# Turning v and the normed scan output on VectorE, in 32x32 blocks that their DRAM stores put in place

## The chip, the cores and the metric

The kernel runs on one core of one Trainium2 chip. The time is device microseconds of one execution of the whole program. Before the change three runs took 1355.96 to 1357.52 us, with a median of 1356.4.

## What is computed

A trunk of two layers runs over 640 tokens, 128 of a prompt and 512 of a latent grid, each 1024 wide. Layer A is a chunked gMLP, layer B a gated DeltaNet in both directions with eight heads, keys and queries of 128 and values of 256. The change lies in layer B. Cut to that, the reference is:

```python
def delta_mixer(h, s0_f, s0_b, w_in, conv_w, A_log, dt_bias, norm_g, w_out):
    proj = h @ w_in
    qkv, z, ab = jnp.split(proj, [2 * KW + VW, 2 * KW + 2 * VW], axis=-1)
    qkv = jax.nn.silu(short_conv(qkv, conv_w))
    q, k, v = jnp.split(qkv, [KW, 2 * KW], axis=-1)
    ...
    o_f, s_f = gated_delta_chunked(q, k, v, g[:, :, 0], beta[:, :, 0], s0_f)
    o_b, s_b = gated_delta_chunked(flip(q), flip(k), flip(v), flip(g[:, :, 1]), flip(beta[:, :, 1]), s0_b)
    o = o_f + flip(o_b)
    o = o * lax.rsqrt(jnp.mean(jnp.square(o), axis=-1, keepdims=True) + LN_EPS) * norm_g
    y = o.reshape(B, N, VW) * jax.nn.silu(z)
    return y @ w_out, s_f, s_b
```

The recurrence wants v with tokens on the partitions; the convolution before it, and the product with z and the output projection behind it, want channels on the partitions. So v and the result o are each turned once on the way.

## The kernel before the change

Layer A takes up to about 500 us of the span, layer B's heads from about 545 to 1245, and layer B's output projection (`out_b`) the rest to 1354, with its first part among the last heads. Products of the two projections are exact to nearly f32: each is three matmuls of split operands, written by `mm3` (L235 high by high, L236 and L237 with the low parts).

Layer B is a set of Python generators, one for each step of a head: `project_head` (one of four 128-channel parts q: 0 is k, 1 is q, 2 and 3 are the halves of v; output in `xp`), `conv` (five taps along the tokens, L845 and L848, then SiLU, L851 and L853; output `cacc`, channels on the partitions), `post_k`, `post_q` and `post_v` (into the layouts that follow), `chunk` (the triangular systems of a 128-token chunk, by products in bank `pt`), `scan` (the recurrence, five steps with a forward and a backward unit each, banks `ps`), `norm_o` (the norm of o), `project_z` and `gate_z` (the gate, and the product with it), `residual`, and the gates.

`stages()` gives every generator a stretch of time, in windows: in window w (-2 to 8) stand the scan of head w, the chunks of head w+1, the projections of head w+2, and the norm and gate of head w-1, each with its begin and end in sixths of a window. `turns()` sorts the pieces by these times, and that is the order in which the code is issued. TensorE and SP (the queue that issues nearly all DMAs) keep this written order; that of VectorE, ScalarE and GpSimd is set by a scheduler. A window is about 80 us long in the profile: the k store of a head (L907) is issued at 804.62, 884.03, 963.48, 1043.96 and 1125.20.

The two steps that the change touches:

- `post_v` (L931): TensorE turns `cacc` into bank `px`, four 128x128 transposes for the latent tokens and one for the prompt (`flip`, L878, which calls `transpose`, L239). ScalarE copies them to `nat` times 0.5 (L938; SiLU was computed without its factor of one half). One store puts `nat` into the DRAM tensor `kvd` (L941), which holds k and v of a head with tokens as rows.
- `norm_o` (L1166) takes the squares of o on ScalarE, and scales o by its norm on GpSimd for heads 0 to 6 (L1182); o has tokens on the partitions. `gate_z` (L1204) then turns each half of o on TensorE, again 4 and 1, and VectorE multiplies `px` by the gate and the norm's weight into `z` (L1213). A store puts the product into `yd` (L1215), from where `out_b` loads it as `cacc` (L1247).

`scan` loads v from `kvd` (L1097, 128 KB each, four buffers), a pair ahead of each step: L1112 is the product of the state S with k and q, L1115 takes it from v, which gives r, L1125 and L1126 are the products with r, L1134 and L1140 the new state and the output. `chunk` loads k as `kn` (L961). Every DMA of SP takes one of eight semaphores in turn, and waits for the DMA that had it before, so at most eight are on their way.

Of the kernel before, what the change touches and what calls it, by code (L numbers as in the profile page):

```python
# [6 lines left out]
F32 = mybir.dt.float32  # L7
# [3 lines left out]
ALU = mybir.AluOpType  # L11
PSUM = bass.MemoryType.PSUM

P = 128
# [33 lines left out]
NORM_LEN = 1.0  # L48
CONV_AT, CONV_LEN, POST_AT, POST_LEN, NORM_AT, GATE_AT, GATE_STEP = 1.0, 1.0, 2.0, 1.0, 0.4, 1.5, 0.6
CAT, CLEN = 0.0, 0.9  # L50
CSTEP = CLEN / 40 * 4
# [22 lines left out]
def tok(c):  # L74
# [7 lines left out]
PIECES = {"scan": 24, "chunk": 40, "norm_o": 4, "gate_z": 4, "conv": 8, "post_k": 13,  # L82
          "post_q": 7, "post_v": 5, "gates": 7, "gates_e": 26, "residual": 17}


def stages():
# [5 lines left out]
    for w in range(-2, H + 1):  # L92
# [11 lines left out]
        for i, (kind, h, q) in enumerate(slots):  # L104
            i = start + i * wide
            add("project_" + kind, (h, q), i / n, (i + wide) / n, 17)
            if kind == "head":
                i += wide - 1
                add("conv", (h, q), (i + CONV_AT) / n, (i + CONV_AT + CONV_LEN) / n)
                add(("post_k", "post_q", "post_v", "post_v")[q], (h, q), (i + POST_AT) / n,  # L110
                    (i + POST_AT + (KLEN if q == 0 else POST_LEN)) / n)
        if w == -2:
# [12 lines left out]
        if at(-1):  # L125
            add("norm_o", (w - 1,), NORM_AT / n, (NORM_AT + NORM_LEN) / n)
            for j in range(2):
                add("gate_z", (w - 1, 4 + j), (GATE_AT + GATE_STEP * j) / n, (GATE_AT + 0.5 + GATE_STEP * j) / n)
    return parts
# [78 lines left out]
class Trunk:  # L208
# [421 lines left out]
    def layer_b(self):  # L630
# [4 lines left out]
        self.e_d = self.dram([P, TT, H, P], "ed")  # L635
        self.kv_d = [self.dram([P, TT, P + DV], "kvd") for _ in range(H)]
        with contextlib.ExitStack() as banks, pool("b_c") as bc:
# [11 lines left out]
            self.convw = t(bc, [P, H, 4, CONV], F32, "convw")  # L649
            nc.sync.dma_start(self.convw, a["convw"])  # L650
            self.ngT = t(bc, [P, 2], F32, "ngT")
            nc.sync.dma_start(self.ngT, a["ngT"])
# [185 lines left out]
    def conv(self, h, q):  # L838

        nc, t = self.nc, self.t  # L840
        xp = self.acc[h, q]
        acc = t(self.b2, [P, PADN], F32, "cacc")
        self.acc[h, q] = acc, xp
        w = self.convw[:, h, q]
        nc.scalar.activation(acc, xp[:, 0:PADN], AF.Copy, scale=w[:, 0:1])  # L845
        yield
        for i in range(1, CONV):
            nc.vector.scalar_tensor_tensor(acc, xp[:, i : i + PADN], w[:, i : i + 1], acc, op0=ALU.mult, op1=ALU.add)  # L848
            yield
        th = xp[:, 2 : 2 + PADN]  # L850
        nc.scalar.activation(th, acc, AF.Tanh, scale=0.5)  # L851
        yield
        nc.vector.scalar_tensor_tensor(acc, th, 1.0, acc, op0=ALU.add, op1=ALU.mult)  # L853
        if q != 1:
            self.gap(xp)
        yield
# [29 lines left out]
    def post_k(self, h, q):  # L886
# [7 lines left out]
        for c0 in (1, 0):  # L894
# [11 lines left out]
            yield  # L906
        nc.sync.dma_start(self.kv_d[h][:, :, 0:P], kn)  # L907
        for c0 in (1, 0):
# [22 lines left out]
    def post_v(self, h, q):  # L931
        nc, t = self.nc, self.t
        s, _ = self.acc[h, q]
        v = t(self.b1, [P, TT, P], F32, "nat")
        for c0 in (1, 0):
            p = self.flip(lambda c: s[:, tok(c)], c0)
            yield
            nc.scalar.mul(v[:, c0 : c0 + p.shape[1], :], p, 0.5)  # L938
            if c0:
                yield  # L940
        nc.sync.dma_start(self.kv_d[h][:, :, P * (q - 1) : P * q], v)  # L941
        yield

    def chunk(self, h, cs):
# [15 lines left out]
        kn = t(b1, [P, nt, P], F32, f"kn{nt}")  # L960
        nc.sync.dma_start(kn, self.kv_d[h][:, those, 0:P])  # L961
        pg = bank()
# [116 lines left out]
    def scan(self, h):  # L1079
# [15 lines left out]
        def load(c):  # L1095
            v = t(b1, [P, DV], F32, "v", bufs=KVB)
            nc.sync.dma_start(v, self.kv_d[h][:, c, P : P + DV])  # L1097
            return v
# [65 lines left out]
    def norm_o(self, h):  # L1164
# [14 lines left out]
        for c in range(TT):  # L1179

            if h < H - 1:
                nc.gpsimd.tensor_scalar(o[c], o[c], f[:, c : c + 1], 0.0, op0=ALU.mult, op1=ALU.add)  # L1182
            elif c % 2:
                nc.vector.tensor_scalar(o[c], o[c], f[:, c : c + 1], None, op0=ALU.mult)
            else:
                nc.scalar.activation(o[c], o[c], AF.Copy, scale=f[:, c : c + 1])
        yield

    def project_z(self, h, q):
# [14 lines left out]
    def gate_z(self, h, q):  # L1204

        nc, t = self.nc, self.t
        z2, o = self.zz[h, q], self.oo[h]
        j = q - 4
        for c0 in (1, 0):
            p = self.flip(lambda c: o[c][:, j * P : (j + 1) * P], c0)  # L1210
            yield
            sl = slice(c0 * P, (c0 + p.shape[1]) * P)
            nc.vector.scalar_tensor_tensor(z2[:, sl], p.rearrange("p c n -> p (c n)"), self.ngT[:, j : j + 1],  # L1213
                                           z2[:, sl], op0=ALU.mult, op1=ALU.mult)
        nc.sync.dma_start(self.y_d[2 * h + j], z2)  # L1215
        yield
# [204 lines left out]
```

## Time and profile before

| what | value |
|---|---|
| runs before, median (lowest to highest) | 1356.4 us (1355.96 to 1357.52) |
| the profiled execution, its own time | 1356.03 us |
| its span | 1354.2 us |
| mean granted TensorE clock | 0.99 |
| transfers: v loads (128 KB) | 72 |
| transfers: stores into `kvd` (320 KB) | 24, of which 16 are v |
| matmul instructions | 8773 |

The time is the span and 1.8 us around it. Rows of the profile have the form "line, engine, operation, output and inputs by the program's names, shapes, count", then the busy time and the mean duration. L240 is the helper that every transpose on TensorE goes through, so these are told apart by what they read: `cacc`, `o` or `nat`. A wait in brackets is the idle time of an engine just ahead of an instruction, and what ended it. In the list of groups, "x128 | 137.7, 1076" reads 128 instructions, 137.7 us of busy time, 1076 ns each.

### The profile page before, as it was taken

How to read it: one execution, taken by the hardware profiler on the slowest of the kernel's cores; microseconds unless marked ns; L12 is line 12 of the kernel's file. 1: busy time of each engine (PE TensorE's matmuls, PEld its weight loads, DVE VectorE, ACT ScalarE, POOL GpSimd, SP SyncE). 2: the span in 40 equal slices, each digit the busy share in tenths (PEclk: the TensorE clock that was granted, in tenths of full speed). 3: DMA queues.
4: the chain of work that ended last, by engine and by line, in shares of the span. 5: the costliest groups of instructions: out<-in, count | busy, mean ns of one | idle time of the engine just before them, and what ended most of it. 6: DMA issues, size and time to landing. Idle time of an engine off the chain costs nothing. (4 is left out here: it accounts for less than half of the span.)

```text
span 1354.2 us, 22812 instructions
## 1 busy us (share of the span) xinstructions
PE 1282.5 (95%) x8773; PEld 1137.3 (84%) x8773; DVE 875.7 (65%) x1655; ACT 578.7 (43%) x1352; POOL 502.0 (37%) x503
## 2 busy tenths in 40 slices
PE   7999999999999999888999999999999999999996
PEld 4688999999997887778888898999899898887785
DVE  4654744444447566798677778686787868656357
ACT  2333522222224334665545354564545546443320
POOL 0221422222223434354343536355464646520024
PEclk9999999999999999998999999999999999999999
DMA  8512233333336324142122422234233242445732
GB/s 337 168 63 93 94 125 125 125 125 125 125 125 218 118 76 145 56 140 86 50 77 73 136 78 65 100 89 153 79 125 108 85 139 88 133 141 174 261 117 78
DMA packets 90254, 163.17 MB, mean 120 GB/s; under 512 B 9089, under 2 KB 55457, under 8 KB 90017
## 3 DMA queue, kind: packets, MB, share of 16 engines
q1 hardware_dynamic: 88704, 156.99, 35.3%
q10 hardware_dynamic: 1440, 4.72, 1.0%
q8 instruction: 69, 1.13, 0.3%
q14 instruction: 41, 0.33, 0.1%
HBM read 135.97 MB, written 25.71 MB: 119 GB/s over the span
## 5 line engine op out<-in xcount | busy, mean ns | idle before, releaser
L231 POOL TENSOR_TENSOR wlo<-wraw,whi 128x256 fp32r<-128x256 f32 (+1 forms) x188 | 194.4, 1054 | 261.6 <-ACT whi L230 261.6
L235 PE MATMUL pp<-hThi,whi 128*128 128x320 f32 (+1 forms) x784 | 280.1, 357 | 0.2 <-ACT hThi L230 0.2
L237 PE MATMUL pp<-hTlo,whi 128*128 128x320 f32 (+1 forms) x784 | 244.7, 312 | 0.4 <-POOL hTlo L231 0.4
L236 PE MATMUL pp<-hThi,wlo 128*128 128x320 f32 (+1 forms) x784 | 244.1, 311 | 0.0
L230 ACT CAST whi<-wraw 128x256 fp32r<-128x256 f32 (+1 forms) x262 | 143.5, 593 | 84.6 <-PE pacc L236 57.6
L235 PE MATMUL pacc<-hThi,whi 128*128 128x320 f32 x512 | 159.6, 312 | 0.0
L237 PE MATMUL pacc<-hTlo,whi 128*128 128x320 f32 x512 | 158.3, 309 | 0.0
L236 PE MATMUL pacc<-hThi,wlo 128*128 128x320 f32 x512 | 158.2, 309 | 0.0
L848 DVE SCALAR_TENSOR_TENSOR cacc<-xp,convw,cacc 128x642 f32<-128x642 f32 x128 | 137.7, 1076 | 25.0 <-ACT cacc L845 23.6
L235 PEld LDWEIGHTS pp<-hThi,whi 128*128 128x128 f32 (+1 forms) x784 | 148.8, 190 | 3.9 <-ACT hThi L230 0.3
L236 PEld LDWEIGHTS pp<-hThi,wlo 128*128 128x128 f32 (+1 forms) x784 | 148.6, 190 | 4.0
L237 PEld LDWEIGHTS pp<-hTlo,whi 128*128 128x128 f32 (+1 forms) x784 | 147.7, 188 | 1.8 <-POOL hTlo L231 0.7
L231 DVE TENSOR_TENSOR wlo<-wraw,whi 128x1024 fp32r<-128x1024 f32 (+1 forms) x74 | 87.7, 1196 | 60.0 <-ACT whi L230 59.5
L248 POOL TENSOR_TENSOR rs<-ve,mhalf 128x1 f32<-128x1 f32 (+2 forms) x39 | 40.1, 1028 | 170.1 <-DVE ve L246 166.7
L235 PEld LDWEIGHTS pacc<-hThi,whi 128*128 128x128 f32 x512 | 96.1, 188 | 3.1 <-issue 2.2
L236 PEld LDWEIGHTS pacc<-hThi,wlo 128*128 128x128 f32 x512 | 96.1, 188 | 0.0
L237 PEld LDWEIGHTS pacc<-hTlo,whi 128*128 128x128 f32 x512 | 96.1, 188 | 0.0
L256 POOL TENSOR_SCALAR gsq<-gsq 128x320 f32<-128x320 f32 (+1 forms) x52 | 27.7, 532 | 138.4 <-ACT gsq L255 137.4
L257 DVE TENSOR_TENSOR gsq<-pacc,gsq 128x320 f32<-128x320 f32 (+1 forms) x52 | 29.1, 565 | 73.9 <-POOL gsq L256 73.8
L255 ACT ACTIVATE gsq<-pacc 128x320 f32<-128x320 f32 (+1 forms) x52 | 25.7, 498 | 106.2 <-PE pacc L237 102.3
L235 PE MATMUL pacc<-whi,hThi 128*128 128x512 f32 x160 | 63.1, 406 | 7.6 <-ACT whi L230 4.4
L1032 ACT CAST TU<-pt 128x512 f16<-128x512 f32 (+1 forms) x120 | 57.2, 525 | 26.4 <-PE pt L1029 25.5
(333 smaller groups left out, 2974.9 us busy)
## 6 DMA issues: line engine op xcount, KB each, us to landing
wraw<-in_w_b SPq DMA_DIRECT2D x48, 512.0 KB
wraw<-in_w_ada SPq DMA_DIRECT2D x37, 512.0 KB
wraw<-in_w_uz SPq DMA_DIRECT2D x32, 512.0 KB
v<-kvd SPq DMA_DIRECT2D x72, 128.0 KB
wraw<-in_a_wo SPq DMA_DIRECT2D x16, 512.0 KB
wraw<-in_b_wo SPq DMA_DIRECT2D x16, 512.0 KB
kvd<-nat SPq DMA_DIRECT2D x24, 320.0 KB
cacc<-yd SPq DMA_DIRECT2D x24, 320.0 KB
```

The costliest lines, as they stand in the source:

```text
L230: self.nc.scalar.copy(hi, src)
L231: (e_lo or self.nc.vector).tensor_tensor(lo, src, f32(hi), op=ALU.subtract)
L235: mm(out, l_hi, r_hi, start=start, stop=False)
L236: mm(out, l_lo, r_hi, start=False, stop=False)
L237: mm(out, l_hi, r_lo, start=False, stop=stop)
L248: nc.gpsimd.tensor_tensor(r, ve, self.mhalf[:, 0:n], op=ALU.pow)
L255: nc.scalar.activation(sq, u, AF.Square)
L256: nc.gpsimd.tensor_scalar(sq, sq, GB, 1.0, op0=ALU.mult, op1=ALU.add)
L257: nc.vector.tensor_tensor(sq, u, sq, op=ALU.mult)
L848: nc.vector.scalar_tensor_tensor(acc, xp[:, i : i + PADN], w[:, i : i + 1], acc, op0=ALU.mult, op1=ALU.add)
L1032: nc.scalar.copy(part, p.rearrange("p s k t (j b) -> p s (k t j) b", b=b))
```

## The change

v is turned by VectorE. Its instruction turns each 32x32 block in place in the grid of blocks, so a block's inside is right and its place is not; the store to DRAM puts the blocks in their places, 32 partitions by 20 blocks by 32 numbers, four stores for each half of v. The half that ScalarE applied is moved into the convolution's weights (one GpSimd operation at the start), and the scale of the tanh is doubled for it. `kvd` is laid out with a token's k and v in one row. The stores stand five pieces behind the transposes, and `post_v` is stretched from 1.0 to 1.4 sixths of a window.

For heads 0 to 6 the norm of o scales on ScalarE instead of GpSimd. A new step `turn_o` turns each o (128x256) with one VectorE instruction, and three pieces later writes it to a new DRAM tensor `od` with four stores (32 partitions by 8 by 32). A new step `load_o` reads it back as `oT`, channels on the partitions, in two loads of 320 KB. `gate_z` is moved from 1.5 to 4.7 sixths of the window, is one VectorE operation of 640 columns out of SBUF, and stores `yd` three pieces later. Head 7 keeps the transposes on TensorE.

```diff
+TURN_AT, TURN_LEN, LOAD_AT, TURNED_AT, VLEN = 1.6, 1.6, 3.7, 4.7, 1.4
...
+            at_gate = GATE_AT
+            if w < H:
+                add("turn_o", (w - 1,), TURN_AT / n, (TURN_AT + TURN_LEN) / n)
+                add("load_o", (w - 1,), LOAD_AT / n, (LOAD_AT + 0.4) / n)
+                at_gate = TURNED_AT
...
-        nc.scalar.activation(th, acc, AF.Tanh, scale=0.5)
+        nc.scalar.activation(th, acc, AF.Tanh, scale=0.5 if q < 2 else 1.0)
...
     def post_v(self, h, q):
...
-        v = t(self.b1, [P, TT, P], F32, "nat")
-        for c0 in (1, 0):
-            p = self.flip(lambda c: s[:, tok(c)], c0)
-            yield
-            nc.scalar.mul(v[:, c0 : c0 + p.shape[1], :], p, 0.5)
-            if c0:
-                yield
-        nc.sync.dma_start(self.kv_d[h][:, :, P * (q - 1) : P * q], v)
+        v = t(self.b1, [P, NT], F32, "nat")
+        nc.vector.transpose(v[:, P:NT], s[:, tok(1).start : tok(4).stop])
+        yield
+        nc.vector.transpose(v[:, 0:P], s[:, tok(0)])
+        for _ in range(5):
+            yield
+        rows = self.kv_d[h].rearrange("(a i) n -> i a n", i=32)
+        for b in range(4):
+            at = P * (q - 1) + 32 * b
+            nc.sync.dma_start(rows[:, :, at : at + 32],
+                              v[32 * b : 32 * b + 32].rearrange("p (a n) -> p a n", n=32))
...
-            if h < H - 1:
-                nc.gpsimd.tensor_scalar(o[c], o[c], f[:, c : c + 1], 0.0, op0=ALU.mult, op1=ALU.add)
-            elif c % 2:
+            if h == H - 1 and c % 2:
...
+    def turn_o(self, h):
...
+        for c in range(TT + 3):
+            if c < TT:
+                x = self.t(self.b0, [P, DV], F32, "ot", bufs=4)
+                nc.vector.transpose(x, o[c])
+                wait.append(x)
+            if c >= 3:
+                cols = self.o_d[h].rearrange("(b j) n -> j b n", j=32)
+                for a in range(4):
+                    at = (c - 3) * P + 32 * a
+                    nc.sync.dma_start(cols[:, :, at : at + 32],
+                                      wait[c - 3][32 * a : 32 * a + 32].rearrange("p (b n) -> p b n", n=32))
+            yield
+
+    def load_o(self, h):
+        self.turned = []
+        for j in range(2):
+            x = self.t(self.b0, [P, NT], F32, "oT", bufs=2)
+            self.nc.sync.dma_start(x, self.o_d[h][j * P : (j + 1) * P, :])
+            self.turned.append(x)
+            yield
...
     def gate_z(self, h, q):
...
+        if h < H - 1:
+            nc.vector.scalar_tensor_tensor(z2, self.turned[j], self.ngT[:, j : j + 1], z2, op0=ALU.mult, op1=ALU.mult)
-        for c0 in (1, 0):
+        for c0 in (1, 0) if h == H - 1 else ():
...
+        if h < H - 1:
+            yield
+            yield
+            yield
         nc.sync.dma_start(self.y_d[2 * h + j], z2)
```

What the change does to the order of SP, in a steady window (head 4's scan loads `kvd_4838`, while head 5's v is written to `kvd_4839`; `wraw` is a weight, `rn` and `x` belong to the residual). Before:

```order
L1097 DMA v_10920<-kvd_4838 128x256
L1097 DMA v_10922<-kvd_4838 128x256
L961 DMA kn_2046_10938<-kvd_4839 128x2x128
L701 DMA x_80_498<-rn_10805 128x256
L696 DMA rn_11020<-n_76_494 128x256
L941 DMA kvd_4839<-nat_10914 640x1x128
L1215 DMA yd_4823<-z_1739_9573 128x640
L166 DMA wraw_11095<-in_w_b 128x1024
L701 DMA x_81_499<-rn_11020 128x256
L1097 DMA v_11155<-kvd_4838 128x256
L1097 DMA v_11157<-kvd_4838 128x256
```

The same place of SP in the changed kernel, from the first of these v pairs to the second:

```order
L1110 DMA v_10930<-kvd_4838 128x256
L1110 DMA v_10932<-kvd_4838 128x256
L974 DMA kn_2039_10948<-kvd_4839 128x2x128
L710 DMA x_80_498<-rn_10821 128x256
L953 DMA kvd_4839<-nat_10743 32x20x32 x4
L705 DMA rn_11027<-n_76_494 128x256
L172 DMA wraw_11099<-in_w_b 128x1024
L710 DMA x_81_499<-rn_11027 128x256
L1214 DMA od_4845<-ot_11049 32x8x32 x4
L953 DMA kvd_4839<-nat_10928 32x20x32 x4
L1110 DMA v_11163<-kvd_4838 128x256
L1110 DMA v_11165<-kvd_4838 128x256
```

Between the pairs stand twelve small stores, where one of `kvd` and one of `yd` stood; the first store of v has moved here from ahead of the first pair, and the `yd` store has gone to the end of the window.

In window 7 (the scan of the last head, loads from `kvd_4841`) TensorE's order holds matmuls of the output projection between those of the scan; `pp` and `pt` with `kq`, `G` and `whi` or `wlo` are the projection, `ps` the scan. Before, around its fourth step:

```order
L236 MATMUL pt_14139<-whi_13814,G_2782_14170 128x512
L1125 MATMUL ps_14040<-r_14034,G_2687_13898 128x256
L1126 MATMUL ps_14040<-r_14034,G_2687_13898 128x256
L1125 MATMUL ps_14043<-r_14037,G_2687_13898 128x256
L1126 MATMUL ps_14043<-r_14037,G_2687_13898 128x256
L237 MATMUL pt_14139<-wlo_13815,kq_14148 128x512
L1112 MATMUL ps_14056<-S_14046,kq_12584 128x256 x2
L1112 MATMUL ps_14059<-S_14049,kq_12584 128x256 x2
L235 MATMUL pt_14140<-whi_13814,kq_14148 128x512
```

The changed kernel's TensorE at the same step, its first rows:

```order
L1138 MATMUL ps_14077<-r_14059,G_2680_13950 128x256
L1139 MATMUL ps_14077<-r_14059,G_2680_13950 128x256
L241 MATMUL pp_14208<-whi_13865,kq_14218 128x512
L1125 MATMUL ps_14090<-S_14080,kq_12622 128x256 x2
L1125 MATMUL ps_14093<-S_14083,kq_12622 128x256 x2
L242 MATMUL pp_14208<-whi_13865,G_2778_14240 128x512
L243 MATMUL pp_14208<-wlo_13866,kq_14218 128x512
L241 MATMUL pt_14209<-whi_13865,kq_14218 128x512
L242 MATMUL pt_14209<-whi_13865,G_2778_14240 128x512
L243 MATMUL pt_14209<-wlo_13866,kq_14218 128x512
```

The products with S are here followed by 26 matmuls of the projection, of which five are shown, before the products with r of the same step; before the change two or three stood there. On SP, 16 stores of `od` stand between the v pair of this step and that of the step ahead.

More of the change, by code (lines that the diff above doesn't have):

```diff
@@ L82 @@
 PIECES = {"scan": 24, "chunk": 40, "norm_o": 4, "gate_z": 4, "conv": 8, "post_k": 13,
-          "post_q": 7, "post_v": 5, "gates": 7, "gates_e": 26, "residual": 17}
+          "post_q": 7, "post_v": 7, "turn_o": 8, "load_o": 2, "gates": 7, "gates_e": 26, "residual": 17}
 def stages():
@@ L110, in stages @@
                 add(("post_k", "post_q", "post_v", "post_v")[q], (h, q), (i + POST_AT) / n,
-                    (i + POST_AT + (KLEN if q == 0 else POST_LEN)) / n)
+                    (i + POST_AT + (KLEN, POST_LEN, VLEN, VLEN)[q]) / n)
         if w == -2:
@@ L126, in stages @@
             add("norm_o", (w - 1,), NORM_AT / n, (NORM_AT + NORM_LEN) / n)
+            at_gate = GATE_AT
[3 more added lines that the diff above has]
+                at_gate = TURNED_AT
             for j in range(2):
-                add("gate_z", (w - 1, 4 + j), (GATE_AT + GATE_STEP * j) / n, (GATE_AT + 0.5 + GATE_STEP * j) / n)
+                add("gate_z", (w - 1, 4 + j), (at_gate + GATE_STEP * j) / n, (at_gate + 0.5 + GATE_STEP * j) / n)
     return parts
@@ L635, in layer_b @@
         self.e_d = self.dram([P, TT, H, P], "ed")
-        self.kv_d = [self.dram([P, TT, P + DV], "kvd") for _ in range(H)]
+        self.kv_d = [self.dram([NT, P + DV], "kvd") for _ in range(H)]
+        self.o_d = [self.dram([DV, NT], "od") for _ in range(H - 1)]
         with contextlib.ExitStack() as banks, pool("b_c") as bc:
@@ L650, in layer_b @@
             nc.sync.dma_start(self.convw, a["convw"])
+            nc.gpsimd.tensor_scalar(self.convw[:, :, 2:4], self.convw[:, :, 2:4], 0.5, 0.0, op0=ALU.mult, op1=ALU.add)
             self.ngT = t(bc, [P, 2], F32, "ngT")
@@ L906, in post_k @@
             yield
-        nc.sync.dma_start(self.kv_d[h][:, :, 0:P], kn)
+        nc.sync.dma_start(self.kv_d[h].rearrange("(c p) n -> p c n", p=P)[:, :, 0:P], kn)
         for c0 in (1, 0):
@@ L960, in chunk @@
         kn = t(b1, [P, nt, P], F32, f"kn{nt}")
-        nc.sync.dma_start(kn, self.kv_d[h][:, those, 0:P])
+        nc.sync.dma_start(kn, self.kv_d[h].rearrange("(c p) n -> p c n", p=P)[:, those, 0:P])
         pg = bank()
@@ L1096, in load @@
             v = t(b1, [P, DV], F32, "v", bufs=KVB)
-            nc.sync.dma_start(v, self.kv_d[h][:, c, P : P + DV])
+            nc.sync.dma_start(v, self.kv_d[h][c * P : (c + 1) * P, P : P + DV])
             return v
@@ L1187, in norm_o @@
         yield
+    def turn_o(self, h):
+        nc = self.nc
+        o = self.oo[h]
+        wait = []
+        for c in range(TT + 3):
[17 more added lines that the diff above has]
+            yield
     def project_z(self, h, q):
```

## The prediction

> **What bounds the kernel now.** I read the page first: its head and the busy shares say how much of the span TensorE, VectorE and the others work.
>
> ```profile
> span 1354.2 us, 22812 instructions
> PE 1282.5 (95%) x8773; PEld 1137.3 (84%) x8773; DVE 875.7 (65%) x1655; ACT 578.7 (43%) x1352; POOL 502.0 (37%) x503
> ```
>
> TensorE is busy for 95% of the span, so time is lost or won by what it is given to do. Those shares are a mean over different stages, so I next asked for busy times by stretch, cut at the length of one window of layer B (one head's scan, with the chunks of the next head and the projections of the one after).
>
> ```profile
> core 0: us, PE busy (x) PEld busy (x) DVE busy (x) ACT busy (x) POOL busy (x), PEclk, DMA share, GB/s
> 800.00:880.00 80.00, 78.04 (x623) 72.50 (x622) 60.46 (x129) 41.45 (x119) 36.08 (x42) 1.00 0.28 91
> 960.00:1041.00 81.00, 77.62 (x618) 72.27 (x619) 60.81 (x128) 41.72 (x120) 45.61 (x52) 1.00 0.34 109
> sum 610.00, PE 583.27 PEld 535.12 DVE 447.24 ACT 308.49 POOL 282.99; mean PE 72.91 PEld 66.89 DVE 55.91 ACT 38.56 POOL 35.37
> ```
>
> In a window TensorE idles 2 to 3.4 us of 80. VectorE has 60.8 us of 81 (75%), ScalarE half, the transfers a third. A matmul taken away here is time taken away, as long as nothing else starts to be waited for. Third, the list of what TensorE waits for, over the whole span (total us, times, longest):
>
> ```profile
> PE px L240 <- DVE cacc L853: 8.0, 4, 4.4
> PE pt L1047 <- ACT U L1038: 4.6, 6, 1.6
> PE ps L1112 <- DVE o L1140: 3.9, 5, 1.2
> PE pt L1029 <- DVE Y L1022: 3.2, 5, 0.6
> PE px L240 <- DVE z L1213: 0.7, 2, 0.5
> ```
>
> The largest wait in it stands before transposes that the change removes: TensorE waits for the convolution's output `cacc` so as to turn it. The rest are short, and all in the scan and the chunks.
>
> **TensorE's part.** The order shows 150 transposes fewer on TensorE: 80 of `cacc` for v (8 heads, two halves, 4 and 1) and 70 of `o` (heads 0 to 6, two halves, 4 and 1). The rows of the bank `px` that they fill, minimum, median and maximum in ns:
>
> ```profile
> L240 PE MATMUL px<-ident,cacc x120: 270/272/474, 575.3 to 1160.4; 128*128 128x128 f32 x120
> L240 PE MATMUL px<-ident,o x80: 270/272/331, 763.1 to 1245.1; 128*128 128x128 f32 x80
> L938 ACT ACTIVATE nat<-px x32: 257/438/602, 598.6 to 1160.9; 128x512 f32<-128x512 f32 x16, 128x128 f32<-128x128 f32 x16
> ```
>
> The 272 ns are from start to end of one; TensorE overlaps them, so the price is the distance between starts. TensorE's timeline around one group of four and one single transpose:
>
> ```profile
> 1009.26 0.31 PE L236 MATMUL pp<-hThi,wlo 128*128 128x320 f32 x1
> 1009.41 0.31 PE L237 MATMUL pp<-hTlo,whi 128*128 128x320 f32 x1
> 1009.55 0.60 PE L240 MATMUL px<-ident,o 128*128 128x128 f32 x4
> 1009.91 0.39 PE L235 MATMUL pp<-hThi,whi 128*128 128x320 f32 x1
> 1010.14 0.30 PE L236 MATMUL pp<-hThi,wlo 128*128 128x320 f32 x1
> ...
> 1011.12 0.31 PE L237 MATMUL pp<-hTlo,whi 128*128 128x320 f32 x1
> 1011.27 0.27 PE L240 MATMUL px<-ident,o 128*128 128x128 f32 x1
> 1011.30 0.39 PE L235 MATMUL pp<-hThi,whi 128*128 128x320 f32 x1
> 1011.53 0.31 PE L236 MATMUL pp<-hThi,wlo 128*128 128x320 f32 x1
> ```
>
> An undisturbed step from one start to the next is 0.15 us (1009.26 to 1009.41). From the L237 ahead of the four to the L236 behind them there are two such steps and the four transposes: 1010.14 - 1009.41 = 0.73, less 0.29 for the two steps. Around the single one it is 1011.53 - 1011.12 = 0.41, less 0.29. Four cost 0.44, one 0.12, a group of five 0.55. Thirty groups (16 of v, 14 of o) make 16.5 us, all of it on the engine that sets the pace. The Trainium skill ("VectorE: DVE Perf Modes", The three transpose paths) gives 390 ns for a 128x128 bf16 transpose on TensorE. By that figure 150 of them would be an estimated 58 us; the rows here, at 0.11 us each between its neighbours, decide.
>
> The waits for `cacc` and for z, 8.0 and 0.7 us, stand before transposes of these two kinds, and nearly all of it goes from TensorE with them. But what follows then comes earlier, and waits for the same `cacc` chain through the v store, or for ScalarE and VectorE in chunk and scan. I take half: 4 us. The ends are 0 and 8.7.
>
> **VectorE's part.** No row of before shows its 32x32 transpose; the nearest are its operations of the same widths:
>
> ```profile
> L853 DVE SCALAR_TENSOR_TENSOR cacc<-xp,cacc 128x642 f32<-128x642 f32 x32 | 27.8, 868 | 7.4 <-ACT xp L851 7.4
> L1140 DVE TENSOR_TENSOR o<-o,ps 128x256 f32<-128x256 f32 x72 | 29.9, 416 | 6.0 <-PE ps L1126 4.3 <-ACT r L1131 1.3
> L1213 DVE SCALAR_TENSOR_TENSOR z<-px,ngT,z 128x512 f32<-128x512 f32 x14 | 10.5, 750 | 7.3 <-PE px L240 7.1
> L1213 DVE SCALAR_TENSOR_TENSOR z<-px,ngT,z 128x128 f32<-128x128 f32 x13 | 4.5, 344 | 0.5 <-PE px L240 0.5
> L1118 ACT ACTIVATE o<-ps,scal 128x256 f32<-128x256 f32 x32 | 14.6, 474 | 49.3 <-DVE r L1115 49.3
> L1182 POOL TENSOR_SCALAR o<-o,rs 128x256 f32<-128x256 f32 x35 | 19.0, 559 | 0.7
> ```
>
> Per window: two times 0.75 + 0.34 for v, five times 0.42 for o, and the product with z in one operation of 640 (0.87 at most, as L853) for 0.75 + 0.34, twice: 2.2 + 2.1 - 0.4 = 3.9 us more, 60.8 to 64.7 of 79. ScalarE gains five of 0.47 for the norm and loses the two L938 pairs (a median of 0.44 each, 1.8 in all): half a microsecond more of 41.7. GpSimd loses five of 0.56. VectorE's 3.9 us in eight windows are 31 us; of a VectorE delay TensorE sees only what falls ahead of an operation it waits for. The ends are 0 and 31; its rows of waits for VectorE that stay (3.9 and 3.2) are about 1% of 610, but the delays come in the same stretches, so I take a tenth: 3 us.
>
> **SP's part.** SP issues the transfers in a written order. Per v half, four stores of 32 partitions by 20 by 32 (128-byte pieces) take the place of one; per head 20 stores of `od` and two loads come new. SP's timeline with VectorE's use of what is loaded, and from the chain of waits the time of one store and one v load:
>
> ```profile
> 1002.29 0.53 SPq L941 DMA_DIRECT2D kvd<-nat  x1
> 1004.94 0.33 SPq L1215 DMA_DIRECT2D yd<-z  x1
> 1006.90 0.96 SPq L1097 DMA_DIRECT2D v<-kvd  x2
> ```
>
> ```profile
> 1012.89 0.48 DVE L1115 SCALAR_TENSOR_TENSOR r<-ps,neg,v 128x256 f32<-128x256 f32 x1 [0.82 <-PE ps L1112]
> ```
>
> ```profile
> 1043.96 3.94 DMA kvd<-nat
> ...
> 1213.43 3.60 DMA v<-kvd
> ```
>
> A v pair issued at 1006.90 is used at 1012.89, 6.0 us later, and 3.6 are its landing: 2.4 us to spare. In the new order four `od` and four `kvd` stores stand ahead of that pair, where one store of `kvd` and one of `yd` stood: by the rows 8 x 0.53 = 4.2 us of issue for 0.9. Between the first two rows SP had nothing to issue for 2.1 us, so issue alone sets the pair back by 4.2 - 0.9 - 2.1 = 1.2, within the 2.4. Over a window 28 more transfers (6 for v, 20 stores and 2 loads of `od`) take 9 to 15 us of SP's 80. What is queued behind a store that waits for VectorE are v pairs and weights, and the weights are asked for well ahead. I take 0 for the steady windows; the other end is the last of the rivals.
>
> **The end of the scan.** In window 7 no more heads follow, and 16 of the `od` stores of head 6 stand in one row between two v pairs of the last scan:
>
> ```profile
> 1218.70 0.93 SPq L1097 DMA_DIRECT2D v<-kvd  x2
> 1223.32 2.05 SPq L1097 DMA_DIRECT2D v<-kvd  x4
> ```
>
> ```profile
> 1254.46 0.24 PE pt L237
> ...
> 1261.12 8.00 DMA cacc<-yd
> ```
>
> Before, four v loads went out together at 1223.32. Now two of them stand behind 16 stores: 5.3 us at 0.33, 8.5 at 0.53. The written order on TensorE puts 26 matmuls of the output projection there (`pp` and `pt` with L235 to L237), 0.24 each, so 6.2 us. What is left, and the reload of `o` before head 6's product, costs between 0 and 8 us; I take 3, because the next load for the output projection stands behind the same 16 stores.
>
> **The sum.** The profiled execution took 1356.03 us, 1.8 beyond its span; the median of the runs is 1356.4. 1356.0 - 16.5 - 4 + 3 + 3 = 1341.5, and 0.4 for the median: 1342. A measurement of this kernel can tell 0.2%, 2.7 us, from no change: faster is below 1353.7, slower above 1359.1.
>
> **The rivals.**
>
> *Better.* All 8.7 us of the waits go, VectorE and the end cost nothing: 1356.4 - 16.5 - 8.7 = 1331. For it: the steady windows show no wait at all before these transposes, so little has to be paid back there. Against: 97% busy leaves short chains of VectorE and ScalarE just hidden. Chance 0.10; with parts of it, 1331 to 1336.
>
> *VectorE becomes what TensorE waits for.* If the transpose costs three times the rows above, a window's v and o transposes take 13 us in place of 4.3, and VectorE is at 73 of 79. It has 20 us free in a window, so it alone sets the pace only from about five times. At three times, a sixth of the extra 8.6 us on the path in each of eight windows gives back 11: 1353, 1346 to 1360. Against: it reads and writes as many elements as its neighbours. Chance 0.10. The page named above gives 311 ns for 128x128 bf16 on VectorE, for blocks of 32x32; that is an estimated 1.24 us for 512 wide, 1.7 times the row taken here, and by it the sum would be near 1344. No run yet shows it.
>
> *The end gives it back.* Scan 7 and the reload of head 6's `o` each go through 16 stores at 0.53; if the output projection runs dry behind them, 8 + 4 us instead of 3: 1351. For it: the last row above, where the end already waits 8 us for a load of that projection. Chance 0.10.
>
> *Slower: the small stores hold SP.* No store of 128-byte pieces stands in the trace beside these; the page only counts small packets:
>
> ```profile
> DMA packets 90254, 163.17 MB, mean 120 GB/s; under 512 B 9089, under 2 KB 55457, under 8 KB 90017
> ```
>
> The change adds 64 x 640 and 140 x 256 pieces of 128 bytes, 76,800, for 10,240 of 512 bytes. Each transfer waits for the one eight before it, so at most eight are on their way. So a v pair goes out at the earliest one landing after the first of the eight stores ahead of it; with a landing of L us instead of the 4.2 that their issue takes, it is set back by 1.2 + (L - 4.2). The point from which that decides, with 2.4 to spare, is L = 5.4, where the row above has 3.9 for a store. Two v pairs of a window have such a block ahead, in seven windows: at 6.5 they lose 14 x 1.1 = 15 us against the gain of 14.5, and 1357 comes out; at 7.1, 24 us and 1366; at 8, 36 us and 1378. Against it: the DMA share of the windows is 0.28 to 0.34, so there is room for as many packets again. Chance 0.18, 1355 to 1380, with its middle at 1366. The Trainium skill ("DMA: Bandwidth & Descriptors", Specifications) asks for at least 512 B a transfer and says that below this a read-modify-write takes place. That speaks for this rival; no run yet shows a time for it.
>
> **How the numbers follow.** The forecast's own case, 1337 to 1346, has 0.52. Better 0.10, VectorE 0.10, the end 0.10, SP 0.18. The likeliest gives 1342. The range 1333 to 1358 leaves out half of the better case and three quarters of SP's: 0.05 + 0.13 = 0.18. Faster by over 0.2%: 0.52 + 0.10, of the end 0.08, of VectorE 0.06, and 0.01 of SP, 0.77. Within 0.2%: 0.02 + 0.03 + 0.03 = 0.08. Slower: 0.14 of SP and 0.01 of VectorE, 0.15.
>
> **What would show it.** Right: windows of about 78 us instead of 80 with TensorE's busy time down by 2, no px wait for `cacc` L853 but the k ones, VectorE near 65 us a window, its 512-wide transpose near 0.7 us, and SP's v pairs still issued 5 us ahead of use. Wrong: transposes on VectorE over 1.5 us for 512 columns; waits of VectorE for v (L1110) in each window; windows of 80 us with TensorE at 75; or a span from the last scan's start to the end that is more than 5 us longer. If the stores land in 2 to 4 us, the slower rival falls.

## The result, and the profile after

The changed kernel takes 1403.5 us (1403.13 to 1404.52), the kernel before 1356.2 in the same runs: a ratio of 1.0345, interval 1.0329 to 1.0362. It is 47 us slower, where 1342 was forecast. First the page's head, as before the change:

```profile
span 1401.3 us, 22752 instructions
PE 1290.9 (92%) x8623; PEld 1138.2 (81%) x8623; DVE 889.2 (63%) x1708; ACT 579.7 (41%) x1355; POOL 490.7 (35%) x469
```

TensorE has its 150 instructions fewer and is busy for 8 us longer. The list of its waits says where it stands idle, and the next rows what the new VectorE operations cost (count, busy time, mean ns):

```profile
PE ps L1138 <- ACT o L1131: 19.9, 7, 4.0
PE pt L1030 <- DVE TU L1017: 18.2, 9, 5.6
PE pt L1060 <- DVE U L1054: 9.9, 6, 2.1
```

```profile
L1208 DVE STREAM_TRANSPOSE ot<-o 128x256 f32<-128x256 f32 x35 | 14.9, 432 | 4.1 <-ACT o L1197 4.1
L1247 DVE SCALAR_TENSOR_TENSOR z<-oT,ngT,z 128x640 f32<-128x640 f32 x12 | 12.8, 1067 | 0.0
L945 DVE STREAM_TRANSPOSE nat<-cacc 128x512 f32<-128x512 f32 x16 | 11.3, 704 | 0.0
L947 DVE STREAM_TRANSPOSE nat<-cacc 128x128 f32<-128x128 f32 x16 | 4.6, 285 | 0.0
```

The wait for `cacc` ahead of the transposes is gone, and three others took its place: before the scan's products with r, and in the chunk before the product with TU and before that with U (two steps of the triangular systems). Each transpose costs about what the operations of the same width cost before (432 ns for 416, 704 for 750, 285 for 344). To see where the time went, I cut the span at the k stores of heads 3 and 7 (`nat` to `kvd`, 804.62 and 1125.20 before):

```profile
810.02 0.37 SPq L916 DMA_DIRECT2D kvd<-nat  x1
...
1156.74 0.37 SPq L916 DMA_DIRECT2D kvd<-nat  x1
```

Up to the first, the change has lost 5.4 us; over the four steady windows between them 26.1 (346.7 for 320.6); behind the second 15.6 (244.6 for 229.0). A steady window is followed on three engines. SP first, from a store of the residual to the second v pair of head 4's scan:

```profile
1021.07 0.32 SPq L710 DMA_DIRECT2D x<-rn  x1
1021.44 1.93 SPq L1214 DMA_DIRECT2D od<-ot  x4
1023.47 2.08 SPq L953 DMA_DIRECT2D kvd<-nat  x4
1025.60 1.01 SPq L1110 DMA_DIRECT2D v<-kvd  x2
```

Before the change the pair went out 0.4 us behind `x<-rn`, now 4.5 us behind it. By the trace's DMA events it landed at 1028.0 and 1028.4. The stores were not held by the limit of eight transfers: the DMA that had the first v load's semaphore before it had landed at 1023.1, 2.5 us before that load was issued. They follow `x<-rn`, for which SP had stood idle since 1013.2, because it waits for GpSimd's `rn`. SP's waits for it over the whole span (total us, times, longest), before and after:

```profile
SPq L701 <- POOL rn L700: 35.5, 9, 4.8
SPq L710 <- POOL rn L709: 81.4, 12, 11.1
```

By itself this wait need not cost anything: in the run below that loads v ahead of the stores (e_ahead) it is 107.6 us, and the windows are 20 us shorter. What is new is that eight stores stand between it and the pair. VectorE then:

```profile
1025.45 0.43 DVE L1208 STREAM_TRANSPOSE ot<-o 128x256 f32<-128x256 f32 x1
1031.31 0.95 DVE L1035 TENSOR_TENSOR Y<-pt,wm 128x128 f16<-128x128 f32 x3 [5.42 <-PE pt L1030]
1034.44 3.08 DVE L857 SCALAR_TENSOR_TENSOR cacc<-xp,convw,cacc 128x642 f32<-128x642 f32 x3 [2.18 <-ACT cacc L854]
1037.44 0.86 DVE L1128 SCALAR_TENSOR_TENSOR r<-ps,neg,v 128x256 f32<-128x256 f32 x2
```

VectorE idles for 7.6 us (5.42 and 2.18), about 5 of them with v there, and takes r 9 us after v landed, behind three Y and three convolution taps. The products with S, which r needs too, were done by 1027.5. So it is the order of VectorE's queue and not the data. Before the change the two r of this step (the first at 1012.89, shown in the prediction) ran ahead of those Y and taps:

```profile
1013.75 0.48 DVE L1115 SCALAR_TENSOR_TENSOR r<-ps,neg,v 128x256 f32<-128x256 f32 x1 [0.38 <-PE ps L1112]
1017.55 0.95 DVE L1022 TENSOR_TENSOR Y<-pt,wm 128x128 f16<-128x128 f32 x3 [3.31 <-PE pt L1017]
```

The scheduler has put them ahead of r. I take it that it reckons v late behind the small stores; what it reckons is not shown, but r stands in its old place in the runs that load v earlier (e_ahead) or have large stores (e_big).

TensorE, whose order is written by hand, stands before the product with r for the last 4.0 us of that time, and pays twice. Its row of the timeline, then the windows table, which has the granted clock in the column behind POOL; the first stretch lies ahead of the same wait one window earlier, the second behind it, the third begins within the wait of this row and ends 4.7 us behind it:

```profile
1038.47 1.22 PE L1138 MATMUL ps<-r,G 128*128 128x256 f32 x2 [4.04 <-ACT o L1131]
```

```profile
940.00:946.70 6.70, 6.70 (x75) 6.16 (x73) 0.95 (x3) 3.20 (x9) 0.65 (x1) 1.00 0.55 115
951.20:954.40 3.20, 3.20 (x10) 2.54 (x9) 2.33 (x4) 0.74 (x1) 1.88 (x2) 0.50 0.11 36
...
1036.60:1043.20 6.60, 4.73 (x13) 4.01 (x14) 5.62 (x10) 1.60 (x3) 4.18 (x5) 0.50 0.45 127
```

At these waits of 4 us the clock is 0.50 for some 3.4 and 6.8 us, and so busy time grows where work has shrunk. A shorter wait can do it too, as an earlier window of the kernel before shows: the row of the wait, then a stretch ahead of it and one behind it.

```profile
715.33 0.22 PE L1028 MATMUL pt<-Y,TU 128*128 128x64 f16 x2 [1.76 <-DVE Y L1022]
```

```profile
709.00:713.00 4.00, 4.00 (x34) 3.72 (x34) 3.50 (x6) 2.95 (x10) 2.97 (x4) 1.00 0.00 0
716.30:719.70 3.40, 3.40 (x15) 3.36 (x15) 1.68 (x6) 2.07 (x5) 0.54 (x1) 0.50 0.27 73
```

But not every such wait is followed by it: behind one of 2.21 us that ended at 925.08 in the changed kernel (before the product with TU), the clock stays at 1.00 from 925.1 to 929.0. Over the span the withheld clock is 0.025 x 1401 = 35 us against 0.01 x 1354 = 14. The Trainium skill ("TensorE: Matmul & The Clock Gate", What's actually happening) has the clock halved after an idle window of some 3.4 us; the length agrees with the stretches here, but a wait of 1.76 us was followed by it and one of 2.21 us was not.

### The profile page after: what moved, and what is told of

It reads as the page before. It is cut to its first block, busy times and chain, and to the rows that moved or that the text cites. A ratio compares the mean times of both kernels' runs of the same rounds, so it can differ in the third digit from the quotient of the medians.

```text
span 1401.3 us, 22752 instructions
## 1 busy us (share of the span) xinstructions
PE 1290.9 (92%) x8623; PEld 1138.2 (81%) x8623; DVE 889.2 (63%) x1708; ACT 579.7 (41%) x1355; POOL 490.7 (35%) x469
## 4 chain that ended last, share of the span: by engine, by line
PE 25%; DVE 15%; issue 7%; ACT 6%; POOL 3%; DMA 2%; SPq 1%; ACTq 0%; POOLq 0%; DVEq 0%
DVE cacc L857 5%; PE pp L241 5%; PE pp L242 4%; PE pp L243 4%; PE ps L1125 2%; POOL rs L254 2%; PE ps L1139 2%; DVE M L995 2%; PE ps L1138 1%; POOL wlo L237 1%; ACT junk L885 1%; ACT cacc L854 1%; PE pt L1030 1%; DVE grhs L805 1%; DMA v<-kvd 1%
## 5 line engine op out<-in xcount | busy, mean ns | idle before, releaser
L237 POOL TENSOR_TENSOR wlo<-wraw,whi 128x256 fp32r<-128x256 f32 (+1 forms) x188 | 199.3, 1081 | 322.7 <-ACT whi L236 308.9
L1035 DVE TENSOR_TENSOR Y<-pt,wm 128x128 f16<-128x128 f32 (+1 forms) x144 | 47.9, 373 | 60.6 <-PE pt L1030 60.3
L1125 PE MATMUL ps<-S,kq 128*128 128x256 f32 x256 | 67.2, 404 | 7.4 <-issue 3.5
```

Of the source, the lines that this page charges most:

```text
L237: (e_lo or self.nc.vector).tensor_tensor(lo, src, f32(hi), op=ALU.subtract)
L1035: nc.vector.tensor_tensor(yc, pair(p), pair(self.wm[:, l - 1, :, 0:nt]), op=ALU.mult)
L1125: nc.tensor.matmul(p[:, q], kq[:, c, q, :], S, start=True, stop=True)
```

## The experiments

Times are medians beside the kernel before on the same chip, with the ratio's interval. The parts of the span are those above: to head 3's k store, the four windows, and the rest; they are of the one profiled execution, which can lie 4 us from the median. Seven runs leave out part of the work or put blocks in wrong places, as their texts say (e_big, e_none, e_stores, e_tiny, e_vbig, e_obig, e_none_mp), and serve for their times alone. The code cuts are shortened.

| run | us | ratio | to head 3 | four windows | rest |
|---|---|---|---|---|---|
| before | 1356.2 | 1 | 804.6 | 320.6 | 229.0 |
| changed | 1403.5 | 1.0329 to 1.0362 | 810.0 | 346.7 | 244.6 |
| e_pin | 1388.5 | 1.0221 to 1.0267 | 805.7 | 337.3 | 245.4 |
| e_big | 1369.7 | 1.0078 to 1.0121 | 807.7 | 319.7 | 236.7 |
| e_v | 1368.9 | 1.0062 to 1.0112 | 808.5 | 322.0 | 237.6 |
| e_o | 1364.7 | 1.0039 to 1.0080 | 806.8 | 319.8 | 236.4 |
| e_none | 1351.4 | 0.9948 to 0.9991 | 803.1 | 315.0 | 231.5 |
| e_dve | 1362.4 | 1.0035 to 1.0079 | 808.3 | 322.5 | 232.3 |
| e_stores | 1419.1 | 1.0445 to 1.0485 | 812.4 | 358.4 | 247.4 |
| e_ahead | 1378.9 | 1.0143 to 1.0221 | 806.5 | 327.0 | 242.8 |
| e_tiny | 1409.3 | 1.0378 to 1.0412 | 817.7 | 350.6 | 241.6 |
| e_vbig | 1373.1 | 1.0096 to 1.0157 | 804.3 | 326.6 | 240.5 |
| e_obig | 1378.7 | 1.0144 to 1.0180 | 811.7 | 329.5 | 238.2 |
| e_actq | 1395.9 | 1.0277 to 1.0313 | 813.0 | 337.9 | 243.8 |
| e_none_mp | 1332.3 | 0.9824 to 0.9858 | 795.6 | 309.0 | 226.0 |
| e_mp | 1369.3 | 1.0086 to 1.0118 | 800.7 | 327.7 | 235.6 |
| e_ahead_mp | 1352.2 | 0.9969 to 0.9997 | 797.8 | 311.3 | 240.5 |
| e_fix2 | 1346.4 | 0.9906 to 0.9945 | 798.9 | 312.1 | 235.5 |
| e_fix3 | 1345.9 | 0.9915 to 0.9954 | 798.4 | 312.4 | 233.0 |
| e_bahead | 1353.1 | 0.9969 to 0.9998 | 803.9 | 318.9 | 228.0 |

**Order alone, large stores, and each half.** My theory was the order on VectorE (A); its rivals transport (B) and VectorE's load (C). The first run pins the order, the second takes the small stores away, the others make one half of the change.

```diff
+    # e_pin: for each VectorE instruction traced after an r
+    add_manual_dep(ins, last_r.name, NoSync)
-    # e_big: the four stores of a group, for v and for o alike
+    nc.sync.dma_start(kv_d[h].rearrange("(c p) n -> p c n", p=P)[...], v.rearrange("p (c n) -> p c n", n=P))
```

Expected of e_pin:

> The changed kernel with one constraint on VectorE's order: nothing that is written behind an r of the scan (the subtraction from v) may be queued ahead of it. Every instruction and every transfer stays. Theory A (order): the scheduler reckons the small stores slow, expects v late, and queues six Y operations and three convolution taps ahead of r in the second scan step; v had in fact landed 8 to 9.5 us before r ran. Then this kernel gets back most of the 47 us: under 1365, and TensorE's waits of 4 us before the products with r (L1138) go. Theory B (transport): the small stores hold SP and the v pairs go out late; then r waits for v in the same place, and the time stays over 1390. Theory C (VectorE's load): the transposes themselves are in the way; over 1390 as well, without waits for v.

Expected of e_big:

> The changed kernel with each group of four stores of 128-byte pieces replaced by one store of 512-byte pieces of the same bytes (the blocks' placing is left out, so v and o are computed from misplaced blocks). VectorE's transposes, the reload of o and all else stay; VectorE's order comes out as before the change around r. Theories A and B: 1335 to 1355, since both the order and the transfers are put right. Theory C: over 1390.

Expected of e_v:

> Only the v part of the change: o is turned on TensorE and scaled on GpSimd as before. In the second scan step r is queued behind six Y operations and no convolution tap. TensorE saves 16 groups, 8.8 us. Theory A: some of the waits before the products with r, 1350 to 1370. Theory B: eight small stores per window instead of 28, 1350 to 1365. The two differ little here; the run is for the shares.

Expected of e_o:

> Only the o part of the change: v is turned on TensorE and stored at once, as before. The r of each scan step is queued where it stood before the change. TensorE saves 14 groups, 7.7 us. Theory A: 1345 to 1360. Theory B: the 20 od stores of each window are most of the small stores and stand ahead of v pairs: 1375 to 1395.

The pin gives back 15 of 47 us. 1388.5 lies between the ranges of A and B, so A alone falls short. VectorE's timeline of that run shows why:

```profile
940.14 0.88 DVE L1140 SCALAR_TENSOR_TENSOR r<-ps,neg,v 128x256 f32<-128x256 f32 x2 [4.57 <-DMA v<-kvd]
```

With r first in the queue, v is really late: both theories hold part. Without small stores (e_big) the four windows are back at 319.7, but the whole stays 14 us slower than before, where both had foreseen 1335 to 1355. Each half alone (e_v at 1368.9, within A's range; e_o at 1364.7, in neither) is level with before in the windows (322.0, 319.8), though it takes transposes off TensorE, while both together lose 26. In the windows of either half VectorE never waits for v; so it seems that a pair behind four small stores still arrives in time, and one behind eight does not.

**One component at a time.** From here on the question was also why the runs without that loss win nothing.

```diff
-            p = self.flip(lambda c: s[:, tok(c)], c0)       # e_none
+            p = s[:, tok(1).start : tok(4).stop] if c0 else s[:, tok(0)]
+        nc.vector.transpose(extra[:, P:NT], s[:, ...])      # e_dve
+                wait.append(o[c])                           # e_stores: stores, no VectorE transposes
-                kv = load(c) if c else prompt or load(c)    # e_ahead
+                kv = coming[n] if coming else prompt or load(c)
+            coming = [load(c) for c, _ in STEPS[i + 1]]
```

Expected of e_none:

> The kernel before, with only the removal: TensorE's 150 transposes are left out, ScalarE copies v unturned out of SBUF, and the gate's product of heads 0 to 6 takes z in place of the turned o (so v and o are left unturned). No transpose on VectorE and no small store. Theory P (TensorE sets the pace, as the prediction had it): 1356 - 16.5, and the px waits with it, 1332 to 1342. Theory D (the chunk's VectorE steps were only just hidden, and TensorE now waits for them, as the two half changes and the run with large stores suggest, which have 4 to 7 us of new waits in four windows): 1345 to 1353.

Expected of e_dve:

> The kernel before with VectorE's 67 transposes added into spare tiles; everything of before stays, TensorE's transposes too, and no small store is added. This is VectorE's load alone, 30 us in all. Theory C (this load is what costs): 1375 or more. Theory of order and transport: 1357 to 1366.

Expected of e_stores:

> The kernel before with the small stores and the reload added, at the places that the change gives them: four 128-byte-piece stores for each v half instead of one, 20 for each o, two loads back; turned on TensorE as before, nothing turned on VectorE (v lands in misplaced blocks, the reloaded o is not used). r of the second scan step is again queued behind Y operations and a convolution tap. Theory of order and transport: 1380 to 1400, more than all the rest of the change together. Theory C: 1357 to 1366.

Expected of e_ahead:

> The changed kernel whole, with one edit: the scan loads each v pair one step ahead, so that the pairs stand in front of the small stores that held them. VectorE's order around r comes out as before the change. Theory of order and transport: the 16 to 26 us that the four steady windows lost come back, and about 12 us of the end with them, 1358 to 1372. Theory C: over 1390.

The small stores alone (with the reload), on the kernel before, cost 63 us, more than the whole change and 19 beyond the range; why they cost more without the rest stays open. VectorE's load alone costs 7, which ends theory C. Putting the v loads ahead of the stores (e_ahead) brings back 25, 7 short of its range. And leaving out TensorE's transposes, with nothing in their place (e_none), brings 4 us of 16.5, as D had it. TensorE's largest wait in layer B is then:

```profile
PE pt L1017 <- DVE TU L1004: 15.7, 9, 5.6
```

**What it is in the stores.** Issue and order (I) against the transfers (T), and a count against a threshold.

```diff
-            nc.sync.dma_start(rows[:, :, at : at + 32], v[32 * b : 32 * b + 32]...)
+            nc.sync.dma_start(rows[0:1, :, at : at + 32], v[32 * b : 32 * b + 1]...)   # e_tiny
+            nc.scalar.dma_start(rows[:, :, at : at + 32], ...)                        # e_actq
+        # e_vbig, e_obig: the large store of e_big for v alone, for o alone
```

Expected of e_tiny:

> The changed kernel with each small store cut to one of its 32 partitions (20 or 8 pieces of 128 bytes instead of 640 or 256; kvd and od are filled with zeros in 15 stores at the beginning of layer B, and nearly all of v and o is left out). The order of SP, of VectorE and of TensorE is word for word that of the changed kernel, and so is the number of transfers; only their size goes. Theory I (issue and order: SP's time for each store, and r queued late on VectorE): 1385 to 1405, and TensorE's waits before L1138 stay. Theory T (the transfers: 76,800 packets on the DMA engines, eight in flight): 1365 to 1375.

Expected of e_vbig:

> The changed kernel with large stores for v alone (one of 512-byte pieces in misplaced blocks), small ones for o: 20 small stores in each window instead of 28. On SP four od stores and one of v stand ahead of the second v pair, not eight; r is queued on VectorE as before the change. If the loss grows with the number of small stores: 1370 + 20/28 of 34, about 1394. If it comes only where a block of stores is longer than the pair's slack (threshold): 1365 to 1378.

Expected of e_obig:

> The changed kernel with large stores for o alone (five of 512-byte pieces in each window, misplaced blocks), small ones for v: eight small stores in each window. One od store and four of v stand ahead of the second v pair; r is queued behind three more Y operations, and behind no convolution tap. By the number of small stores: 1370 + 8/28 of 34, about 1380. By the threshold: 1368 to 1380, with TensorE's waits before L1138 at 5 us or less in all.

Expected of e_actq:

> The changed kernel whole, with the small stores issued by ScalarE instead of SP; the transfers and their sizes stay. SP's v pairs are no longer behind stores, and r is queued early on VectorE. ScalarE gains some 28 issues of about 0.5 us in a window, 14 us on 40 of 80. Theory I (SP's issue and the order): the steady windows come back to about 80 us, 1365 to 1385, with what ScalarE's load costs on top. Theory T: stays over 1395.

With 1/32 of the small stores' bytes and packets, and the same order on SP, VectorE and TensorE, the loss is all there, and 6 us more (e_tiny). In that run SP's rows (minimum, median, maximum ns of one issue) and TensorE's wait are:

```profile
L1221 SPq DMA_DIRECT2D od<-ot x140: 599/599/1060, 768.6 to 1282.7; - x140
```

```profile
PE ps L1145 <- ACT o L1138: 18.4, 7, 4.0
```

An issue takes 0.6 us however little it moves (0.45 with all its pieces). So the price is SP's time, where the stores stand ahead of v, and what the scheduler makes of it; T falls. The run with small stores for o alone (e_vbig) came out at 1373, as the threshold has it and not the count (1394). That with small stores for v alone (e_obig), 1379, fits both, and its waits before the product with r were 10.0 us where I had said 5. The threshold is not sharp: the windows are 6.9 and 9.8 us longer in these two than with large stores only (319.7), and 27 with all the small ones. The run on ScalarE's queue (e_actq) missed: at 1395.9 it is 11 us above theory I's range and just on T's side. TensorE no longer waits before the products with r there, but 22.4 us for TU and 9.9 for Y, which VectorE makes, and 6.7 for what ScalarE makes of TU; I take these to be the price of the issues on ScalarE, which no run shows alone. Against T stands e_tiny.

**Where the removed TensorE time went.** The place can be seen in the kernel before, on VectorE and on TensorE between the transpose of A (L1002) and the first product with TU (L1017):

```profile
993.44 2.61 DVE L982 SCALAR_TENSOR_TENSOR M<-pe,beta,masks 128x128 f32<-128x128 f32 x2
995.97 0.41 DVE L1140 TENSOR_TENSOR o<-o,ps 128x256 f32<-128x256 f32 x1
996.30 0.91 DVE L982 SCALAR_TENSOR_TENSOR M<-pe,beta,masks 128x128 f32<-128x128 f32 x1
997.12 0.41 DVE L1004 TENSOR_TENSOR TU<-pt,wm 128x256 f16<-128x256 f32 x1
```

```profile
992.76 0.29 PE L1002 MATMUL pt<-id,A 128*128 128x128 f16 x2
...
994.26 0.60 PE L240 MATMUL px<-ident,cacc 128*128 128x128 f32 x4
...
997.84 0.23 PE L1017 MATMUL pt<-TU,A 128*128 128x64 f16 x2
```

TensorE comes to the product with TU 0.3 us after VectorE has made it, with the transposes of `cacc` among what it does meanwhile. VectorE has the M products, needed late, ahead of TU. The edit queues them behind it. It also gives `pe`, from which M is made, a second buffer for groups of two chunks; no run has that alone:

```diff
-        pe = t(b1, [P, nt, P], F32, f"pe{nt}")
+        pe = t(b1, [P, nt, P], F32, f"pe{nt}", bufs=nt)
+    for i, c in enumerate(cs):          # the M products, moved behind TU in the code
+        ins = nc.vector.scalar_tensor_tensor(M[:, i, 1 + d], pe[:, i], ...).ins
+        self.tc.add_manual_dep(ins, tu.name, NoSync)
```

Expected of e_none_mp:

> The run without TensorE's 150 transposes (and without the turning), with one constraint: VectorE's four M products of a chunk (L982, 0.7 us each) are queued behind the chunk's TU product instead of ahead of it. In the run without it TensorE waited 15.7 us for TU in nine places, each followed by half clock. Theory W (that wait is where the removed TensorE time went): the TU waits fall under 6 us and the time to 1340 to 1347. Otherwise (the time is given back wherever it is taken, since VectorE's and ScalarE's chain binds the window): 1348 to 1353, with other waits in their place.

Expected of e_mp:

> The kernel before with the same constraint alone (M behind TU), transposes on TensorE as they were. Before, TensorE waited 4.1 us for TU in two places. Theory W: 1351 to 1355, at most the 4 us and their half clock. Otherwise 1355 to 1358.

Expected of e_ahead_mp:

> The changed kernel with both repairs: v pairs loaded one step ahead of use, and M queued behind TU. Without the second it took 1379 us, with 20.2 us of waits for TU. Theory W: 10 to 18 us less, 1360 to 1369. Otherwise within 5 us of 1379. Neither expects it under the kernel before: VectorE's load costs 7 us and the removal brought 4.

One reading in the first of these texts is wrong: of the nine waits for TU only the three of 5.6, 2.8 and 2.8 us stood at half clock; behind the five of 0.83 us the granted clock stayed at 1.00. Without transposes and with that order (e_none_mp) it takes 1332 us, 22.5 less than before, where the prediction's sum had 20.5 for the transposes and their waits; it is more than I expected here. TensorE's waits and two windows of it:

```profile
PE pt L1021 <- DVE TU L1002: 2.5, 3, 1.2
```

```profile
800.00:880.00 80.00, 78.75 (x631) 73.65 (x630) 64.69 (x131) 43.79 (x124) 40.53 (x44) 1.00 0.33 105
1041.00:1121.00 80.00, 78.03 (x616) 72.57 (x616) 63.81 (x132) 44.13 (x127) 46.61 (x53) 1.00 0.35 110
```

A window is 77.2 us long on average (309.0 / 4), and VectorE is at 64 of 80 without harm. The control surprised: with TensorE's transposes kept (e_mp), the same edit costs 14 us, outside both ranges. Its list shows a wait that I had not foreseen:

```profile
PE px L240 <- DVE z L1217: 15.6, 7, 3.6
```

TensorE turns o into the one `px` bank, VectorE must empty it with the z product, and M now stands ahead of that: in one such place three M products run up to 921.8, the z product follows, and TensorE's next transpose of o starts at 922.5 after 2.7 us of waiting. So the transposes tie TensorE to VectorE's queue, and with them the early place of M is the better one (1355 us against 1369). With both repairs the changed kernel (e_ahead_mp) takes 1352 us, just under the kernel before; "Neither expects it under" was wrong.

**The end.**

Expected of e_fix2:

> The changed kernel with both repairs (v one step ahead, M behind TU), and with head 6 turned on TensorE as before the change, so that no small store stands in the last scan's window. The run with head 6 turned on VectorE lost 11.5 us behind its last k store against the kernel before, with 16 od stores taking 7.8 us of SP between two v pairs and loads of the output projection behind them. Theory I (SP's issue) for the end: 6 to 11 us come back, 1341 to 1347, faster than both kernels. If the end is lost for another reason: 1350 to 1355.

Expected of e_fix3:

> As the run before it, with heads 5 and 6 both turned on TensorE. Window 6 has no projections of a new head to hide small stores behind, so its stores may cost as well; if they do, 2 to 4 us less than with head 6 alone, 1339 to 1344; if not, 1 to 3 us more, for five transposes more on TensorE that VectorE's z product ties to it.

Expected of e_bahead:

> Control: the kernel before with the v pairs loaded one step ahead, and nothing else. Nothing waits for v in its steady windows (VectorE waited 1.0 us for v in the whole execution), so 1353 to 1357 by every theory.

e_ahead_mp has still 11.5 us too many behind head 7's k store. On SP and TensorE it shows:

```profile
1212.06 7.84 SPq L1221 DMA_DIRECT2D od<-ot  x16
1219.94 0.92 SPq L1114 DMA_DIRECT2D v<-kvd  x2
1220.90 0.43 SPq L1297 DMA_DIRECT2D cacc<-yd  x1
```

```profile
1257.75 0.83 PE L241 MATMUL pp<-whi,hThi 128*128 128x512 f32 x2 [4.31 <-ACT hThi L236]
```

Turning head 6 on TensorE again (e_fix2) brings 6 us, 5 of them in this part: 1346.4, 0.7% faster than the kernel before (0.55 to 0.94%). It is the fastest kernel here that leaves nothing out, along with its neighbour with heads 5 and 6 (e_fix3), which can't be told from it. The rest of the end's loss, 4.0 to 6.5 us, stays open. Its largest waits of TensorE are one of 4.0 us for v at the start of the last scan in e_fix2 and one of 3.9 for z in e_fix3; and e_big, without small stores, is 7.7 us over in this part too, so not all of the loss is theirs. Loading v ahead without the change (e_bahead) gives some 3 us (0.3 to 4.2 by the interval), so it is the two repairs with the change that win, not the loads by themselves.

## Why the prediction was wrong, step by step

- **What bounds the kernel.** "A matmul taken away here is time taken away, as long as nothing else starts to be waited for." The proviso decided, and the sum gave it no price. Removal alone measured 4.2 us for the 20.5 in the sum (16.5 and 4); with VectorE's M products behind TU, an edit that alone costs 14 us, removal and edit together measured 22.5. The price of a transpose was about right: in the four windows of that run TensorE has 80 matmuls fewer and is busy for 10.4 us less (301.0 for 311.5); a stretch of 3.4 us at half clock that is gone accounts for 1.7, which leaves 8.7 where 16 groups at 0.55 make 8.8. That it lay wholly on the path was wrong. TensorE at 97% was no proof of a bound: VectorE was full up to TU, and transposes stood in TensorE's order where it would else have waited for it.
- **VectorE's part.** Forecast 3.9 us more in a window; 2 x (0.70 + 0.29) + 5 x 0.43, and the z product at 1.07 twice for 2.18, make 4.1. On the path 3 was taken, and 6.8 came for the transposes alone (e_dve). The Trainium skill ("VectorE: DVE Perf Modes", The three transpose paths) has 311 ns for 128x128 in bf16; the rows have 285 in f32, and 704 for 512 columns, where four times its figure would be 1.24 us.
- **SP's part, the step that failed most.** "So issue alone sets the pair back by 1.2, within the 2.4 ... I take 0." The gap of 2.1 us was subtracted, but in the new order the stores stand behind `x<-rn`, which waits for GpSimd, so none of them can use it: the pair went out 4.1 us later behind that store, more than the 2.4 to spare. The steady windows, taken at 0, lost 26 us. The small stores cost 63 us by themselves; in the changed kernel, 34 of the 61 us between forecast and result go with them (1403.5 against 1369.7 with large stores).
- **A step that was missing.** The order of VectorE was treated as given. The scheduler moved r of the second scan step behind three more Y and three taps; pinning it gave 15 us. The prediction read only the orders of SP and TensorE.
- **The end.** 3 us were taken, and 15.6 came behind head 7's k store. The third rival had the place, and 12 us. Its cause, head 6's stores, is shown in part: without them 5 of 11.5 us went, and the rest stays open.
- **The slower rival** had place and sign with a chance of 0.18, a price that was too low (1380 at most), and the wrong mechanism. Its point was a landing of 5.4 us; by the trace's events the `od` stores landed in 1.8 us and those of v in 2.3 (medians), so it was the order and the issue and not the landing. The rule on transfers under 512 B (the Trainium skill, "DMA: Bandwidth & Descriptors", Specifications) left no mark in the time: with the small packets all but gone, the loss stayed.

## What to carry to other kernels

Many small DMAs cost their queue's issue time, here 0.45 to 0.7 us each, and moving less made it no shorter; read off what stands behind them in that queue and what in turn waits for it, and put loads that a recurrence needs ahead of stores that nobody waits for. Before you remove work from the busiest engine, look up what the others do in the same microseconds: work that covers a neighbour's full stretch is worth little until that stretch is reordered, here 4 us of 16.5. And where a scheduler sets the order, read the new order of every engine that feeds the chain, since other work may have moved ahead of it.

## What the runs showed of the hardware

- Some waits of TensorE of 1.8 to 4 us came with 3.4 or 6.8 us at a clock of 0.50 (1.76 us before 715.33 in the kernel before; 4.04 before 1038.47 in the changed one), others not (2.21 before 925.08). By these rows a wait that does costs an estimated 1.4 to 2 times its length: half of 3.4 us on 4.04 and on 1.76.
- A 32x32 transpose of f32 on VectorE took 285, 432 and 704 ns for 128, 256 and 512 columns on 128 partitions.
- One DMA issue on SP took 0.60 and 0.69 us where it moved one partition of 8 or 20 pieces, and 0.45 and 0.52 (medians) with 32 partitions: fewer bytes made it no shorter.
